# Own tile for sums of weights, later splits of new operands and next weights split a step ahead, in a one-core decoder layer

## The chip, the cores and the metric

The kernel runs on one core of a Trainium2 chip. The metric is the device time of one execution in microseconds, and the time of a kernel is the median of several executions. The engines named below are PE (matrix products), DVE (elementwise on tensors), ACT (activations, copies and casts), POOL, and SP, whose queue starts most of the DMA transfers. Each engine works through its own instructions strictly in order, and a semaphore holds it where it needs what another engine or a transfer has not yet delivered.

## The reference

One layer of a hybrid decoder for a prompt of 1024 tokens and eight sample tokens that share the weights (together 1032 columns), width 1024, in fp32:

```python
xn = rmsnorm(x, norm_mix_w)
sc_b, sc_c, sc_x, z, xbc, dt, q, gates = split(xn @ w_in)
y_a = (sc_b * conv3(sc_c * sc_x)) @ w_sc_out
y_b = group_rmsnorm((ssd(silu(conv4(xbc)), dt, ...) + D * xs) * silu(z)) @ w_ssm_out
y_c = cross_attention(q, mem_k, mem_v) @ w_attn_o
x = x + (sigmoid(g_a) * y_a + sigmoid(g_b) * y_b + sigmoid(g_c) * y_c) @ w_merge_o
xn = rmsnorm(x, norm_ffn_w)
x = x + (silu(xn @ w_gate) * (xn @ w_up)) @ w_down      # hidden width 2816
y = rmsnorm(x, norm_final_w)
```

For the sample tokens the state-space part (`ssd`) is one step of a recurrence over a state of 32 x 64 x 128 for each of the eight samples, which is read, updated and written back. The memory keys and values, the convolution histories and the states are outputs too.

## The kernel before

Every fp32 operand is split into a high part, which the matrix engine takes without loss, and a low part, the rest. ACT casts the high part (`S.copy`) and DVE subtracts it from the source (`V.tensor_sub`). A product is the sum of three matmuls: high with high, high with low, low with high.

The large matrix products go through `strassen()`, which makes two blocks of 128 output rows in one **step**: instead of eight half products it takes seven, named after the form of the moving operand that each uses: B11, T1, nT2, B21, T3, B22 and T4. Each product is 24 matmuls. The forms are sums of halves of the activations, made and split once and kept in SBUF for many steps. The weights are loaded per step as two raw tiles (`raw1`, `raw2`, by `st_raw`) and split (`st_split`) in four ways: A (raw1 itself, for B11 and B21), S (a first sum, in the tile `sa`, for T1 and nT2), T (a second sum, for T3 and B22) and D (half of raw2, for T4). The second sum is made by `st_adds2`, which writes it over raw1. Three PSUM tiles (m0 to m2) take turns: the copies to SBUF (`first`, L311) and the additions (L359, L371, L374, L381) empty them for the products that follow. In the steps of the first stage and of the hidden layer, a step's outputs are copied by ACT (L311) first.

Steps are named after what they make. In the first stage, C, B, X, G and Z stand for parts of `w_in`'s columns; X steps feed a convolution on DVE, which with its slots runs beside the next G step. The sample states run in the same stage: L859 loads a state tile `st`, L867 scales it on ACT (eight instructions a tile), L869 and L873 update and reduce it on DVE, L881 stores it. In the feed-forward stage, steps g0 to g20 and u0 to u20 make the gate and up halves of the 22 blocks of hidden rows. d00 to d06 and d10 to d16 are the down projection, with the first 1024 hidden rows and then with the second 1024; the last six blocks go another way (h_d).

The forms of the first 2048 hidden rows lie in DRAM (`hf_d`). `h_form` loads one form's two tiles of 128x1032 into event tiles and splits them into the tiles of activations: in u20 for d00 and again in d06 for d10. It is called by `used(f)`, as soon as the product with form f has been written down, since the new form takes the tiles of the old one. Pools: three raw, three high and three low weight tiles, twelve tiles a kind for the activations, five event tiles (`ev`), eight big tiles (which hold the outputs of steps and the residual x3).

The order of instructions on an engine comes from a scheduler that estimates when things are ready, not from the order of the source; `tick()` and `in_turn` only add constraints. Transfers of SP's queue start in order too: one that waits for a buffer holds up those behind it.

## Time and profile before

| | us |
|---|---|
| median of 3 runs | 2505.39 (2504.51 to 2506.88) |
| profiled execution, its own time | 2509.08 |
| its span | 2505.8 |
| PE busy in the span | 2434.5 (97%) |
| DVE busy | 1596.0 (64%) |
| ACT busy | 1070.7 (43%) |

The profiled execution lies 3.28 us above its span and 3.69 us above the median of the three runs. PE's busy time is the sum of its matmuls as the trace models them; the time of a step is read from the start of its first matmul to that of the next step's first one. A row of a timeline has the start in us, the length, the engine, the line, the operation with the tiles it writes and reads, and in brackets how long the engine had been idle and what released it.

### The profile page before, as it was taken

Reading aid. Unit: us, or ns where it says so; the run is one execution under the profiler, and the core shown is the slowest. Engines: PE = TensorE matmul, PEld = TensorE weight load, DVE = VectorE, ACT = ScalarE, POOL = GpSimd, SP = SyncE. Lnnn points to the kernel's source line nnn. Section 1 sums busy time; section 2 is a strip of 40 time slices with the busy share of each in tenths; the row PEclk is TensorE's granted clock in tenths of the full one; section 3 lists DMA queues with packets and bytes.
Section 4 is the critical chain, followed back from the end, with each engine's and each line's share of the span. In section 5 each row is a group of like instructions: output and inputs, shape, how many; then the busy total and the mean of one; then the engine's idle time right before and its main releaser. Section 6 shows DMA issues by size and latency. Waiting matters only on the chain.

```text
span 2505.8 us, 45588 instructions
## 1 busy us (share of the span) xinstructions
PE 2434.5 (97%) x18906; PEld 2315.8 (92%) x18906; DVE 1596.0 (64%) x2598; ACT 1070.7 (43%) x1716; POOL 116.3 (5%) x163
## 2 busy tenths in 40 slices
PE   7999999999999999999999989999999999999998
PEld 5899999999999999888888877899999999989998
DVE  5754586777677674656767562454777556566655
ACT  6554455354545435556544441223443333343222
POOL 0200010000000000221120000000000000000000
PEclk9999999999999999999999999999999999999999
DMA  6345434334344446567878677765444323274321
GB/s 197 106 128 167 131 107 145 114 117 127 124 127 128 134 150 209 171 214 253 265 230 283 202 262 237 263 235 158 149 158 127 110 89 111 68 268 141 100 85 68
DMA packets 356077, 404.80 MB, mean 162 GB/s; under 512 B 16422, under 2 KB 286870, under 8 KB 355863
## 3 DMA queue, kind: packets, MB, share of 16 engines
q1 hardware_dynamic: 335422, 344.18, 44.0%
q10 hardware_dynamic: 20449, 57.71, 5.9%
q8 instruction: 148, 2.42, 0.4%
q14 instruction: 58, 0.48, 0.1%
HBM read 286.74 MB, written 115.32 MB: 160 GB/s over the span
## 4 chain that ended last, share of the span: by engine, by line
PE 56%; DMA 4%; DVE 3%; ACT 1%; issue 1%; SPq 0%; ACTq 0%; DVEq 0%
PE po L214 12%; PE pm L1738 4%; PE ps_q L214 3%; PE pd L214 1%; PE py L981 1%; PE pss L994 1%; PE po L973 1%; PE d00m L260 1%; PE d10m L260 1%; PE Z14m L260 1%; PE G16m L260 1%; PE B6m L260 1%; PE C7m L260 1%; PE d16m L260 1%; PE d14m L260 1%; PE d02m L260 1%
## 5 line engine op out<-in xcount | busy, mean ns | idle before, releaser
L926 ACT ACTIVATE r<-r,acum 128x128 f32<-128x128 f32 x256 | 79.1, 391 | 3.8 <-DMA r<-ac_d 3.3
L867 ACT ACTIVATE st<-st,es 128x128 f32<-128x128 f32 x128 | 41.6, 394 | 61.4 <-DMA st<-in_state_ssm_dram 51.5
L697 DVE SCALAR_TENSOR_TENSOR ax<-u,prm,ax 128x1024 f32<-128x1024 f32 x44 | 56.3, 1280 | 0.0
L958 POOL TENSOR_TENSOR xdd<-xdt,decst 128x512 f32<-128x512 f32 x32 | 38.9, 1216 | 288.3 <-DVE xdt L954 288.3
L1385 DVE TENSOR_TENSOR yr<-po,yr 128x1032 f32<-128x1032 f32 x8 | 9.8, 1231 | 55.9 <-PE po L214 45.9
L977 DVE TENSOR_TENSOR y<-po,ea 128x512 f32<-128x512 f32 x28 | 19.3, 689 | 37.8 <-PE po L973 37.8
L952 DVE TENSOR_TENSOR r<-r,cbm 128x1024 f32<-128x1024 f32 x32 | 39.2, 1224 | 2.4
L869 DVE SCALAR_TENSOR_TENSOR st<-sr,dts,st 128x128 f32<-128x128 f32 x128 | 39.4, 345 | 0.4
L951 ACT COPY bT<-bp 128x128 f32<-128x128 f32 x32 | 8.5, 266 | 69.7 <-DVE cbm L949 69.5
L1950 ACT ACTIVATE fj<-psy 128x512 f32<-128x512 f32 (+1 forms) x18 | 10.7, 596 | 59.0 <-PE psy L1948 58.9
L981 PE MATMUL py<-r,xdt 128*64 128x128 f32 x512 | 35.0, 279 | 0.0
L873 DVE SCALAR_TENSOR_TENSOR sr<-st,sr 128x128 f32<-128x128 f32 x128 | 34.4, 285 | 0.8
L927 ACT ACTIVATE r<-r 128x1024 f32<-128x1024 f32 x32 | 33.8, 1057 | 0.6
L954 DVE TENSOR_TENSOR xdt<-xp,dtT 128x512 f32<-128x512 f32 x32 | 21.9, 684 | 19.0 <-PE xp L947 18.8
L1745 DVE TENSOR_TENSOR x<-pm,xT 128x516 f32<-128x516 f32 x16 | 11.1, 695 | 35.1 <-PE pm L1738 35.1
L994 PE MATMUL pss<-xdd,bT 128*128 128x512 f32 x64 | 33.3, 602 | 0.0
L766 ACT ACTIVATE ax<-ax 128x1032 f32<-128x1032 f32 x22 | 23.5, 1068 | 19.5 <-DVE ax L700 19.4
L981 PEld LDWEIGHTS py<-r,xdt 128*64 128x64 f32 x512 | 27.3, 136 | 4.2 <-issue 0.5
L973 PE MATMUL po<-bc,s 128*128 128x128 f32 x224 | 29.7, 275 | 1.0 <-DVE s L1000 1.0
L1007 POOL TENSOR_TENSOR s<-s,cdec 128x512 f32<-128x512 f32 x28 | 30.2, 1080 | 7.3 <-DVE s L1000 6.6
L973 PEld LDWEIGHTS po<-bc,s 128*128 128x128 f32 x224 | 27.6, 191 | 2.7 <-issue 1.6
L1667 DVE TENSOR_TENSOR gt<-po,gt 128x1032 f32<-128x1032 f32 x8 | 9.8, 1230 | 30.0 <-PE po L214 27.8
(9065 smaller groups left out, 9013.2 us busy)
## 6 DMA issues: line engine op xcount, KB each, us to landing
r<-ac_d SPq DMA_DIRECT2D x32, 512.0 KB
gt<-gt_d SPq DMA_DIRECT2D x24, 516.0 KB
xs_d<-ax ACTq DMA_DIRECT2D x22, 516.0 KB
gt_d<-G ACTq DMA_DIRECT2D x20, 516.0 KB
x<-xs_d SPq DMA_DIRECT2D x16, 516.0 KB
zs<-zs_d SPq DMA_DIRECT2D x16, 516.0 KB
yb_d<-x SPq DMA_DIRECT2D x16, 516.0 KB
in<-yb_d SPq DMA_DIRECT2D x16, 516.0 KB
```

What stands on the lines that cost most here:

```text
L214: PE.matmul(out[:, c : c + n], wt[:, ks], x[:, c : c + n], start=(k == 0 and i == 0), stop=(k == nk - 1 and i == 2),)
L260: PE.matmul(hv(ps)[:, c : c + n], wt[:, ks], x[:, c : c + n], start=(start and kt == 0 and i == 0), stop=(kt == 3 and i == 2), skip_group_ ...
L697: V.scalar_tensor_tensor(acc[:, :T], u[:, j : j + T], w[j], acc[:, :T], op0=ALU.mult, op1=ALU.add)
L867: S.activation(st[:, i], st[:, i], AF.Copy, scale=es[:, g * 4 + i, b : b + 1])
L869: V.scalar_tensor_tensor(st[:, i], rb, dts[:, g * 4 + i, b : b + 1], st[:, i], op0=ALU.mult, op1=ALU.add)
L926: S.activation(r[:, j, :], r[:, j, :], AF.Relu, scale=-1.0, bias=acum[:, c, h : h + 1])
L952: V.tensor_tensor(r, r, bc(cbm.unsqueeze(1), [P, HPG, P]), op=ALU.mult)
L958: G.tensor_tensor(b3(xdd, HPG), b3(xdt, HPG), bc(decst[:, c, hs].unsqueeze(2), [P, HPG, 64]), op=ALU.mult)
L973: PE.matmul(po[:, t * P : (t + 1) * P], state["s"][:, t * P : (t + 1) * P], bcg[1][:, cs], start=True, stop=True,)
L981: PE.matmul(py[hp : hp + 64, (h // 2) * P : (h // 2 + 1) * P], xdt[:, h * 64 : (h + 1) * 64], r[:, (h % 2) * 4 + h // 2, :], start=True, s ...
L994: PE.matmul(pss, bT, xdd, start=True, stop=True)
L1738: PE.matmul(hv(ps)[:, c : c + n], wt[:, ks], x[:, half * HT + c : half * HT + c + n], start=(k == 0 and i == 0), stop=(k == KD - 1 and i = ...
```

## The change

Five parts. (1) `st_adds2` writes the second sum into a tile of its own, `sb`, from the event tiles, and leaves raw1 as it is; the T split reads `sb`. (2) `used(f)` no longer splits at once: `h_form` starts the loads and returns a function that splits, and `turning` keeps these until three more products are done (`LATE`). Those left over at the end of a step are called in the next one. (3) `h_form` loads straight into the tile of the low part, casts the high part from there and subtracts in place; no event tile is taken, and the load waits until PE has read the tile's old content. (4) `following`: u20 and d06 load the first raw tile of the next step (named u20f and d06f) and make its A split (u20F, d06F), and `ahead` hands both to that step. Their D split stands ahead of T3. (5) The product of g20 and u20 with its two stores moves into d00 (`opening`, called as its `hook`), with the instruction that reads PSUM first, and so do four of the eight loads of the residual; the other four are ahead of d00.

```diff
...
 LAG = 3
+LATE = 3
...
         V.tensor_add(sa[:, 512:], sa[:, :512], raw1[:, :512])
         return raw1, raw2, sa, st_split(sa, f"{nm}S")
-    def st_adds2(raw1, raw2, sa):
-
-        V.tensor_add(raw1[:, :512], raw1[:, :512], raw2[:, :512])
+    def st_adds2(raw1, raw2, sa, nm, sums):
+        sb = sums(f"{nm}sb")
+        V.tensor_add(sb[:, :512], raw1[:, :512], raw2[:, :512])
         V.scalar_tensor_tensor(
-            raw1[:, 512:], sa[:, 512:], -1.0, raw1[:, 512:], op0=ALU.mult, op1=ALU.subtract
+            sb[:, 512:], sa[:, 512:], -1.0, raw1[:, 512:], op0=ALU.mult, op1=ALU.subtract
         )
-        return raw1
-
-    def st_sums2(raw1, raw2, sa, nm):
-        return st_split(st_adds2(raw1, raw2, sa), f"{nm}T")
+        return sb
+
+    def st_sums2(*args):
+        return st_split(st_adds2(*args), f"{args[3]}T")
+
+    ahead = []
+    turning = deque()
     def strassen(
-        src1, src2, forms, nm, sums, outs, early=None, after_t3=None, ready=None, hook=None, into=False, refill=None
+        src1, src2, forms, nm, sums, outs, early=None, after_t3=None, ready=None, hook=None, into=False,
+        refill=None, following=None,
     ):
...
                 S.copy(dst, ps)
         def used(f):
-            if refill is not None:
-                refill(f)
-
-
-        if ready is None and early is None:
+            turning.append(refill(f) if refill is not None else None)
+            if len(turning) > LATE:
+                g = turning.popleft()
+                if g is not None:
+                    g()
+
+
+        lead = ahead.pop() if ahead else None
+        if lead is not None:
+            raw1, raw2 = lead[0], st_raw(src2, f"{nm}r2")
+        elif ready is None and early is None:
             raw1, raw2 = st_raw(src1, f"{nm}r1"), st_raw(src2, f"{nm}r2")
...
         o11, o12, o21, o22 = outs()
         if early is None:
             pc = st_ps(tags[2], f"{nm}{tags[2]}")
-            wA = st_split(raw1, f"{nm}A")
+            wA = st_split(raw1, f"{nm}A") if lead is None else lead[1]
             prod(pa, wA, 0, "B11", True)
         else:
             tick()
...
             first(o11, hv(pa))
             used("B11")
         if ready is None:
-            sb = st_adds2(raw1, raw2, sa)
+            sb = st_adds2(raw1, raw2, sa, nm, sums)
...
             freed[0] = V.tensor_tensor(o12, hv(pa), o12, op=ALU.add).ins
         if ready is None:
             wT = st_split(sb, f"{nm}T")
+        if following is not None:
+            raw = st_raw(following, f"{nm}f")
+            wD = st_split(raw2[:, 512:], f"{nm}D", 512)
         tick()
         prod(pa, wT, 0, "T3", False)
         if after_t3 is not None:
...
         V.tensor_tensor(o12, o12, hv(pb), op=ALU.subtract)
         used("B22")
         tick()
-        wD = st_split(raw2[:, 512:], f"{nm}D", 512)
+        if following is None:
+            wD = st_split(raw2[:, 512:], f"{nm}D", 512)
+        else:
+            ahead.append((raw, st_split(raw, f"{nm}F")))
         prod(pa, wD, 0, "T4", False)
         used("T4")
         if into:
...
-    g0 = (*g0, st_sums2(*g0[:3], "g0"))
+    g0 = (*g0, st_sums2(*g0[:3], "g0", ev_sums))
...
         V.scalar_tensor_tensor(t2, t2, -1.0, b21, op0=ALU.mult, op1=ALU.subtract)
         form("T4", kt, t2)
-    def hidden_pair(nm, j, refill=None):
+    def hidden_pair(nm, j, **turn):
         o = []
         e = early.get((nm, j))
...
         src = ffn[nm]
         pa = strassen(
-            ev_sums, outs, e, ready=g0 if (nm, j) == ("g", 0) else None, refill=refill,
+            ev_sums, outs, e, ready=g0 if (nm, j) == ("g", 0) else None, **turn,
         )
         return o[0], o[1], pa if e is None else pa
...
     def h_form(ch, f):
-        for i in range(2):
-            t = ev_tile(f"hf{ch}{f}{i}", (P, 2 * HT))
-            SY.dma_start(t, hf_d[ch, FORMS.index(f), i])
-            mk = fx.get(f) or act_pair
-            hi, lo = mk("ah", f"h{ch}{f}{i}h"), mk("al", f"h{ch}{f}{i}l")
-            split_to(hi, lo, t.rearrange("p (a c) -> p a c", a=2))
+        mk = fx.get(f) or act_pair
+        pairs = [(mk("ah", f"h{ch}{f}{i}h"), mk("al", f"h{ch}{f}{i}l")) for i in range(2)]
+        for i, (hi, lo) in enumerate(pairs):
+            SY.dma_start(f32(lo), hf_d[ch, FORMS.index(f), i].rearrange("p (a c) -> p a c", a=2))
             hforms[ch][f] += [(hi[:, a], lo[:, a]) for a in range(2)]
+
+        def split():
+            for hi, lo in pairs:
+                S.copy(hi, f32(lo))
+                V.tensor_sub(lo, f32(lo), f32(hi))
+
+        return split
+
+    def w_rows(ch, m):
+
+        src = a["w_ffn_down"][0, ch * 1024 : (ch + 1) * 1024, m * P : (m + 1) * P]
+        return src.rearrange("(k t p) c -> p t k c", t=2, p=P)
     hs = {}
     for j in range(0, NF, 2):
...
         S.activation(s1, s1, AF.Silu)
         S.activation(s2[:, HS[1]], s2[:, HS[1]], AF.Silu)
         S.activation(s2[:, HS[0]], pa, AF.Silu, scale=-1.0)
-        u1, u2, pa = hidden_pair("u", j, (lambda f: h_form(0, f)) if j == NF - 2 else None)
-        V.tensor_mul(s1, s1, u1)
-        V.tensor_mul(s2[:, HS[1]], s2[:, HS[1]], u2[:, HS[1]])
-        V.scalar_tensor_tensor(s2[:, HS[0]], pa, -1.0, s2[:, HS[0]], op0=ALU.mult, op1=ALU.mult)
+        turn = dict(refill=lambda f: h_form(0, f), following=w_rows(0, 0)) if j == NF - 2 else {}
+        u1, u2, pa = hidden_pair("u", j, **turn)
+
+        def product(j=j, s1=s1, s2=s2, u1=u1, u2=u2, pa=pa):
+            V.scalar_tensor_tensor(s2[:, HS[0]], pa, -1.0, s2[:, HS[0]], op0=ALU.mult, op1=ALU.mult)
+            V.tensor_mul(s1, s1, u1)
+            V.tensor_mul(s2[:, HS[1]], s2[:, HS[1]], u2[:, HS[1]])
+            if j >= 16:
+                SY.dma_start(h_d[j - 16], s1)
+                SY.dma_start(h_d[j - 15], s2)
+
+        if j == NF - 2:
+            continue
+        product()
         if j >= 16:
-            SY.dma_start(h_d[j - 16], s1)
-            SY.dma_start(h_d[j - 15], s2)
             continue
         b11, b12, b21, b22 = (t[:, c] for t in (s1, s2) for c in HS)
         t1, t3, nt2, t4 = (t[:, c] for t in (u1, u2) for c in HS)
...
         kt = (j % 8) // 2
         for f, t in enumerate((b11, t1, nt2, b21, t3, b22, t4)):
             SY.dma_start(hf_d[j // 8, f, kt // 2][:, (kt % 2) * HT : (kt % 2 + 1) * HT], t)
-    def w_rows(ch, m):
-
-        src = a["w_ffn_down"][0, ch * 1024 : (ch + 1) * 1024, m * P : (m + 1) * P]
-        return src.rearrange("(k t p) c -> p t k c", t=2, p=P)
-
-    for m in range(KD):
-        x2[m] = big(f"x3_{m}")
-        SY.dma_start(x2[m], x2_d[m])
+    def residual(*ms):
+        for m in ms:
+            x2[m] = big(f"x3_{m}")
+            SY.dma_start(x2[m], x2_d[m])
+
+    residual(0, 1, 2, 3)
+
+    def opening():
+        product()
+        residual(4, 5, 6, 7)
+
     for ch in range(2):
         for m in range(0, KD, 2):
+            turn = dict(refill=lambda f: h_form(1, f), following=w_rows(1, 0)) if ch == 0 and m == KD - 2 else {}
             strassen(
                 w_rows(ch, m), w_rows(ch, m + 1), hforms[ch], f"d{ch}{m}", ev_sums,
                 lambda m=m: (x2[m][:, HS[0]], x2[m][:, HS[1]], x2[m + 1][:, HS[0]], x2[m + 1][:, HS[1]]),
-                into=True, refill=(lambda f: h_form(1, f)) if ch == 0 and m == KD - 2 else None,
+                into=True, hook=opening if ch == 0 and m == 0 else None, **turn,
             )
     st_stack.close()
     pmm[0] = ctx.enter_context(tc.tile_pool(name="pmm2", bufs=2, space=PSUM))
```

Three places in the order of instructions follow, rows as they stand before and after. A name with a number is one buffer; x4 means four alike in a row.

The first place is step C0 of the first stage, on ACT. `c` and `su` are its outputs, `st` the state tiles, C0Th and C0Dh the high parts of its T and D splits. Before:

```order
L247 CAST C0Th<-C0r_4649 128x1024
L817 DMA gt_d<-G_4415 128x1032
L311 COPY c_4655<-C0m_4653 128x516
L867 ACTIVATE st_5231<-st_5231,es 128x128 x4
L311 COPY su_4656<-C0m_4654 128x516
L867 ACTIVATE st_5231<-st_5231,es 128x128 x2
L867 ACTIVATE st_5700<-st_5700,es 128x128
L247 CAST C0Dh<-C0r_4651 128x512
L311 COPY c_4655<-C0m_4653 128x516
L867 ACTIVATE st_5700<-st_5700,es 128x128 x7
```

After:

```order
L248 CAST C0Th<-C0sb 128x1024
L834 DMA gt_d<-G_4427 128x1032
L316 COPY c_4668<-C0m_4666 128x516
L884 ACTIVATE st_5247<-st_5247,es 128x128 x4
L316 COPY su_4669<-C0m_4667 128x516
L884 ACTIVATE st_5247<-st_5247,es 128x128 x3
L248 CAST C0Dh<-C0r_4664 128x512
L316 COPY c_4668<-C0m_4666 128x516
L884 ACTIVATE st_5718<-st_5718,es 128x128 x4
```

The D cast and the second copy of c now stand ahead of the first activation on the second state tile; all eight activations of the first state tile are ahead of them.

The same place on SP: the loads of weights C0r, C1r and of the states, and the stores of older ones. Before:

```order
L241 DMA C0r_4651<-in_w_in_dram 128x8x128
L881 DMA out_s_ssm_dram<-st_4457 128x4x128 x2
L859 DMA st_5231<-in_state_ssm_dram 128x4x128
L241 DMA C1r_4863<-in_w_in_dram 128x8x128
L859 DMA st_5231<-in_state_ssm_dram 128x4x128
L881 DMA out_s_ssm_dram<-st_4613 128x4x128 x2
L241 DMA C1r_4865<-in_w_in_dram 128x8x128
L859 DMA st_5700<-in_state_ssm_dram 128x4x128 x2
```

After:

```order
L242 DMA C0r_4664<-in_w_in_dram 128x8x128
L898 DMA out_s_ssm_dram<-st_4470 128x4x128 x2
L242 DMA C1r_4877<-in_w_in_dram 128x8x128
L876 DMA st_5247<-in_state_ssm_dram 128x4x128 x2
L242 DMA C1r_4879<-in_w_in_dram 128x8x128
L898 DMA out_s_ssm_dram<-st_4626 128x4x128 x2
L876 DMA st_5718<-in_state_ssm_dram 128x4x128 x2
```

Both loads of the first state tile now stand behind C1's first weights, and C1's second weights ahead of the stores.

The second place is DVE at the change from u20 to d00. h0... are the splits of the new forms, d00A/u20F the A split, x_0 and x_1 the residual. The piece before starts with the last splits of forms:

```order
L390 TENSOR_TENSOR h0T40l<-hf0T_23851,h0T40h 128x2x516
L390 TENSOR_TENSOR h0T41l<-hf0T_23857,h0T41h 128x2x516
L1850 TENSOR_TENSOR g20o_23374<-g20o_23374,u20o_23581 128x1032
L1851 TENSOR_TENSOR g20o_23375<-g20o_23375,u20o_23582 128x516
L1852 SCALAR_TENSOR_TENSOR g20o_23375<-u20m_23579,g20o_23375 128x516
L248 TENSOR_TENSOR d00Al<-d00r_23884,d00Ah 128x1024
L340 TENSOR_TENSOR d00sa<-d00r_23887 128x512
L341 TENSOR_TENSOR d00sa<-d00sa,d00r_23884 128x512
L293 TENSOR_TENSOR d00r_23884<-d00r_23884,d00r_23887 128x512
L294 SCALAR_TENSOR_TENSOR d00r_23884<-d00sa,d00r_23884 128x512
L248 TENSOR_TENSOR d00Sl<-d00sa,d00Sh 128x1024
```

After, from u20's subtraction of B22 to the next splits:

```order
L388 TENSOR_TENSOR u20o_23642<-u20o_23642,u20m_23641 128x516
L1861 TENSOR_TENSOR h0B211l<-h0B211l,h0B211h 128x2x516
L249 TENSOR_TENSOR d00Sl<-d00sa,d00Sh 128x1024
L1861 TENSOR_TENSOR h0T30l<-h0T30l,h0T30h 128x2x516
L1861 TENSOR_TENSOR h0T31l<-h0T31l,h0T31h 128x2x516
L1880 SCALAR_TENSOR_TENSOR g20o_23435<-u20m_23640,g20o_23435 128x516
L1881 TENSOR_TENSOR g20o_23434<-g20o_23434,u20o_23642 128x1032
L1882 TENSOR_TENSOR g20o_23435<-g20o_23435,u20o_23643 128x516
L1861 TENSOR_TENSOR h0B220l<-h0B220l,h0B220h 128x2x516
L1861 TENSOR_TENSOR h0B221l<-h0B221l,h0B221h 128x2x516
```

and from there, without a gap, to d02's A split:

```order
L314 TENSOR_TENSOR x_0_23906<-d00m_23917,x_0_23906 128x516
L1861 TENSOR_TENSOR h0T40l<-h0T40l,h0T40h 128x2x516
L314 TENSOR_TENSOR x_1_23908<-d00m_23918,x_1_23908 128x516
L1861 TENSOR_TENSOR h0T41l<-h0T41l,h0T41h 128x2x516
L249 TENSOR_TENSOR d00Tl<-d00sb,d00Th 128x1024
L314 TENSOR_TENSOR x_0_23906<-d00m_23917,x_0_23906 128x516
L370 TENSOR_TENSOR x_0_23906<-d00m_23919,x_0_23906 128x516
L249 TENSOR_TENSOR d00Dl<-d00r_23914,d00Dh 128x512
L385 TENSOR_TENSOR x_1_23908<-x_1_23908,d00m_23917 128x516
L388 TENSOR_TENSOR x_0_23906<-x_0_23906,d00m_23918 128x516
L398 TENSOR_TENSOR x_1_23908<-x_1_23908,d00m_23917 128x516
L249 TENSOR_TENSOR d02Al<-d02r_24138,d02Ah 128x1024
```

The A split, d00's sums and its S split have gone ahead of the forms T3 to T4, the product stands in the middle of these splits, and the T split stands at their end. d02's A split stands behind the last subtraction of d00 (L398).

The third place is DVE in step G6, beside the convolution of X6 (ax, L697 to L700 before). Before:

```order
L697 SCALAR_TENSOR_TENSOR ax_6006<-u_5806,prm,ax_6006 128x1024
L698 SCALAR_TENSOR_TENSOR ax_6020<-h_xc,prm,ax_6020 128x8
L700 SCALAR_TENSOR_TENSOR ax_6006<-u_5806,prm,ax_6006 128x1032
L697 SCALAR_TENSOR_TENSOR ax_6020<-u_5807,prm,ax_6020 128x1024
L248 TENSOR_TENSOR G6Tl<-G6r_6031,G6Th 128x1024
L697 SCALAR_TENSOR_TENSOR ax_6020<-u_5807,prm,ax_6020 128x1024
L869 SCALAR_TENSOR_TENSOR st_6092<-sr_6090,dts,st_6092 128x128
L700 SCALAR_TENSOR_TENSOR ax_6020<-u_5807,prm,ax_6020 128x1032
L869 SCALAR_TENSOR_TENSOR st_6092<-sr_6090,dts,st_6092 128x128 x7
```

After:

```order
L714 SCALAR_TENSOR_TENSOR ax_6025<-u_5824,prm,ax_6025 128x1024
L715 SCALAR_TENSOR_TENSOR ax_6039<-h_xc,prm,ax_6039 128x8
L717 SCALAR_TENSOR_TENSOR ax_6025<-u_5824,prm,ax_6025 128x1032
L714 SCALAR_TENSOR_TENSOR ax_6039<-u_5825,prm,ax_6039 128x1024
L294 TENSOR_TENSOR G6sb<-G6r_6050,G6r_6052 128x512
L714 SCALAR_TENSOR_TENSOR ax_6039<-u_5825,prm,ax_6039 128x1024
L295 SCALAR_TENSOR_TENSOR G6sb<-G6sa,G6r_6050 128x512
L717 SCALAR_TENSOR_TENSOR ax_6039<-u_5825,prm,ax_6039 128x1032
L886 SCALAR_TENSOR_TENSOR st_6112<-sr_6110,dts,st_6112 128x128 x5
L249 TENSOR_TENSOR G6Tl<-G6sb,G6Th 128x1024
```

The two sums (sb) come later than the S split, and the T split stands behind the last instructions of the convolution and five updates of a state.

## The prediction

> **What bounds the kernel now.** I read the page's busy times first, then the waits of PE, then windows cut at the starts of single steps, and last the timelines of the engines that PE waits for.
>
> ```profile
> span 2505.8 us, 45588 instructions
> PE 2434.5 (97%) x18906; PEld 2315.8 (92%) x18906; DVE 1596.0 (64%) x2598; ACT 1070.7 (43%) x1716; POOL 116.3 (5%) x163
> ```
>
> PE is busy for 97% of the span, and the change does not alter its number of matmuls. What can be won are PE's stops, 2505.8 − 2434.5 = 71 us in all, and the slow matmuls that follow a long stop. The stops that the change can touch are these (engine, tile and line that waits, what it waits for, us in total, times, longest):
>
> ```profile
> PE d00m L260 <- DVE g20o L1852: 5.9, 1, 5.9
> ...
> PE d10m L260 <- DVE x L381: 3.5, 1, 3.5
> ...
> PE C6m L260 <- ACT c L311: 2.7, 1, 2.7
> ...
> PE C2m L260 <- ACT c L311: 2.0, 1, 2.0
> PE C0m L260 <- ACT c L311: 2.0, 1, 2.0
> PE d10m L260 <- DVE d10Al L248: 2.0, 1, 2.0
> ...
> PE C4m L260 <- ACT c L311: 1.5, 1, 1.5
> ...
> PE X8m L260 <- ACT u L311: 0.4, 1, 0.4
> ...
> PE X12m L260 <- ACT u L311: 0.3, 1, 0.3
> ```
>
> The waits are less than what the stops cost. Windows that run from one step's first matmul to the next one's (columns: window, its length, busy time of PE, weight loads, DVE, ACT and POOL, then granted clock, DMA share, GB/s) are, for u20, d00, d02, d06 and d10:
>
> ```profile
> 2213.04:2232.96 19.92, 19.92 (x170) 19.92 (x169) 17.10 (x17) 17.03 (x20) 0.00 (x0) 1.00 0.87 293
> 2232.96:2262.12 29.16, 23.22 (x171) 22.81 (x169) 21.14 (x26) 6.56 (x8) 0.00 (x0) 0.82 0.69 236
> 2262.12:2282.04 19.92, 19.92 (x170) 19.92 (x169) 11.54 (x15) 3.78 (x4) 0.00 (x0) 1.00 0.18 53
> 2301.97:2321.90 19.93, 19.93 (x171) 19.93 (x169) 18.50 (x20) 15.03 (x15) 0.00 (x0) 1.00 0.85 273
> 2321.90:2350.50 28.60, 23.11 (x170) 22.70 (x169) 20.22 (x25) 6.92 (x7) 0.00 (x0) 0.88 0.22 69
> ```
>
> A step without a stop takes 19.92 us, 2.85 for each of its seven products. d00 takes 29.16, a loss of 9.24 on 5.94 of waiting; d10 takes 28.60, a loss of 8.68 on 5.5. The rest is the clock, 0.82 and 0.88 in these windows. PE's timeline (start, length, then the instruction) shows it at d00:
>
> ```profile
> 2233.20 0.40 PE L260 MATMUL d00m<-h0B110l,d00Ah 128*128 128x256 f32 x2
> 2239.54 0.80 PE L260 MATMUL d00m<-h0B210h,d00Ah 128*128 128x256 f32 x2 [5.94 <-DVE g20o L1852]
> 2240.14 0.63 PE L260 MATMUL d00m<-h0B210l,d00Ah 128*128 128x256 f32 x2
> ```
>
> In the same way for one undisturbed step of the first stage, and C0, C2, C4 and C6:
>
> ```profile
> 402.88:422.87 19.99, 19.99 (x170) 19.99 (x169) 19.26 (x48) 11.45 (x14) 1.07 (x2) 1.00 0.52 159
> 422.87:446.65 23.78, 21.78 (x170) 21.58 (x169) 13.79 (x33) 12.31 (x26) 1.24 (x2) 0.93 0.45 135
> 566.96:589.22 22.26, 20.25 (x171) 20.04 (x169) 13.70 (x33) 12.11 (x27) 1.23 (x2) 1.00 0.49 142
> 710.26:732.00 21.74, 20.24 (x170) 20.04 (x169) 13.70 (x33) 11.85 (x25) 1.23 (x2) 1.00 0.49 146
> 852.50:877.16 24.66, 21.91 (x170) 21.50 (x169) 13.78 (x33) 13.20 (x27) 1.23 (x2) 0.93 0.45 138
> ```
>
> Over 19.99 these lose 3.79, 2.27, 1.75 and 4.67, together **12.48**. C0 and C6, with stops of 2.0 and 2.7, also lose clock (0.93); C4 with 1.5 does not.
>
> **Why C0 waits.** Timelines of ACT, SP and DVE:
>
> ```profile
> 435.00 0.40 ACT L867 ACTIVATE st<-st,es 128x128 f32<-128x128 f32 x1 [5.05 <-DMA st<-in_state_ssm_dram]
> 435.81 0.58 ACT L311 COPY c<-C0m 128x516 f32<-128x516 f32 x1
> 429.76 0.38 SPq L241 DMA_DIRECT2D C1r<-in_w_in_dram  x1
> 430.39 0.93 SPq L859 DMA_DIRECT2D st<-in_state_ssm_dram  x2
> 428.51 1.22 DVE L248 TENSOR_TENSOR C0Tl<-C0r,C0Th 128x1024 fp32r<-128x1024 f32 x1
> ```
>
> The copy of c that lets PE write T3 stands on ACT behind a state activation, which sat 5.05 us for its load. That load stood on SP behind the second load of C1's weights, which waited for a raw tile; and the tile was held until DVE's T split at 428.51 to 429.73 had read it, because the sums of weights lay in it.
>
> **The change: own tile for sums.** The T split now reads the sum tile, so a raw tile comes free two or more us earlier. More surely, ACT's order is turned: in C0 the copy of c and the D cast stand ahead of the first st_5718 activation (before: st_5700 ahead of both). The wait for that load now falls behind the copy, with nothing of this step queued behind it but C1's A cast, needed only at the next step. The other state tile (st_5247) has both its halves loaded behind C1's first weights; it is used ahead of the su copy, and by SP's order its load should land before ACT comes to it. The four places have one pattern, and I take the whole **−12.5** there. Bounds: nothing gained (the other activation inherits the wait), and 12.5. X8 and X12 have the same turn: their waits of 0.4 and 0.3 go, **−0.7**.
>
> What it costs: the sums are two instructions as before, but their tile must come from five event tiles, and DVE's order puts the T split later in X and G steps, the first-stage ones with convolution work. For G2:
>
> ```profile
> 407.36 1.22 DVE L248 TENSOR_TENSOR G2Tl<-G2r,G2Th 128x1024 fp32r<-128x1024 f32 x1
> 409.96 1.28 DVE L700 SCALAR_TENSOR_TENSOR ax<-u,prm,ax 128x1032 f32<-128x1032 f32 x1
> 411.16 2.11 DVE L869 SCALAR_TENSOR_TENSOR st<-sr,dts,st 128x128 f32<-128x128 f32 x7
> 414.77 0.40 PE L260 MATMUL G2m<-xnh,G2Tl 128*128 128x256 f32 x2
> ```
>
> The split ends at 408.58, and PE reads it at 414.77, 6.2 us later. In the new order (the G6 rows of the section on the change) one more convolution instruction, the last one of the convolution, and five state updates stand ahead of it: 1.2 + 1.2 + 5 × 0.3 = 3.9 us. That leaves 2.3 us, so I charge nothing as forecast; what hides it is the products T1 to B21. For small new waits, where such margins are thinner (X0, g0, u0), I set **+0.7** (bounds 0 and 3).
>
> **The change: h splits and d weights.** Before, DVE came to d00 with the splits of h, the product with u20 and only then d00's A split:
>
> ```profile
> 2237.05 1.23 DVE L1850 TENSOR_TENSOR g20o<-g20o,u20o 128x1032 f32<-128x1032 f32 x1
> 2238.19 0.69 DVE L1851 TENSOR_TENSOR g20o<-g20o,u20o 128x516 f32<-128x516 f32 x1
> 2238.80 0.69 DVE L1852 SCALAR_TENSOR_TENSOR g20o<-u20m,g20o 128x516 f32<-128x516 f32 x1
> ```
>
> The starts give DVE's prices: 1.14 for a split or a wide product, 0.6 for half of one. Now u20Fl (the A split) stands far ahead, the STT that frees PSUM comes first of the three product instructions, and the T3, B22 and T4 splits of h fall in d00, whose DVE ends on the T split and the add of x_0 that reads nT2's PSUM (row 1992 of the order). Counted from u20's start: B22 ends at 6 × 2.85 = 17.1. From there to row 1992 stand ten instructions of 1.14 and six of 0.6, 15.0 us, so DVE is done at 32.1, or 32.7 if the first starts 0.6 late. PE comes to T3 after 106 of d00's 168 matmuls, at 19.92 × (1 + 106/168) = 32.5. The STT is done at 17.1 + 5.8 = 22.9 and B21, which needs its PSUM, comes at 19.92 + 5.7 = 25.6. So d00's stop goes from 9.24 lost to about 0.6 (bounds 0 and 2): **−8.6**. It keeps a margin near zero, and what is late next is this DVE chain.
>
> The loads are under it. Each h load now waits until PE has left its tile, two per product. A load alone took:
>
> ```profile
> 2212.54 0.34 SPq L1837 DMA_DIRECT2D hf0nT<-hf_d  x1
> ...
> GB/s 0 0 0 0 0 0 264 116 231 380 380 413 297 33 0 0 66 8 82 195 260 313 326 330 334 154 181 153 252 351 415 297 330 182 248 83 215 248 281 363
> GB/s 0 0 303 427 344 385 385 413 344 372 413 413 330 372 427 413 372 358 372 399 179 14 14 61 38 99 79 82 167 130 154 160 123 160 215 307 341 341 348 376
> ```
>
> (the strips have 40 slices; the first, from 2212, of 0.25 us; the second, from 2115, of 0.15 us and with stores in the same 2064-byte pieces that the new loads use). The load was issued at 2212.54 and had landed by 2215.3, 2.75 us. Two of 528 KB per 2.85 us ask for 371 GB/s, and the second strip shows 330 to 427. Then the last one, T41, issued at about 20.0, lands near 22.9, while DVE, after ten more instructions behind B22, comes to it at 29.2. At 300 GB/s it would land at 27 and x_0 behind it at 28.8, where DVE wants x_0 at 26.9: a stop of some 2 us, the upper bound above.
>
> d10 goes the same way: its A split (d06Fl), sums and S split stand ahead of d10; x_7's last subtraction, for which it waited 3.5, no longer has a split of T4 ahead of it. By the same count d10Tl is done at 30.3 and wanted at 31.8. I leave 0.2 of 8.68: **−8.5** (bounds 0 and 2 of stop).
>
> One wait is new: d02Al now stands behind x_1's last subtraction of d00, which reads T4. T4 ends with d00, 0.6 + 1.2 us later the split is ready, and PE has 8 matmuls, 0.95 us, to do without it. With a semaphore's delay: **+1.3** (bounds 0 and 2). The copies of product and stores moved into d00 are in the count; the loads of x_4 to x_7 queue on SP behind the two stores, and d04 wants them a step later, so they cost nothing.
>
> Sum: −8.6 − 8.5 + 1.3 − 12.5 − 0.7 + 0.7 = **−28.3**. The profiled run took 2509.1, 3.3 around its span, and 3.7 above the median of 2505.4. It gives 2480.8, and by the median **2477**.
>
> **The rule weighed here.** The rows say that a stop of 2.0 us (C0) already cost 3.79, with the clock at 0.93, and 1.5 (C4) only 1.75. The Trainium skill, "TensorE: Matmul & The Clock Gate", Part 1, has the clock fall to half after an idle window of about 3.4 us, free-running. By it the stops of 0.6 and 1.3 that I leave cost themselves alone, as by C4's row, and a stop of 2 us would too, where C0's row makes it 3.8; the row decides.
>
> **Rivals.** *The state wait only moves (0.2).* st_5247's activation, which stands ahead of the su copy, inherits C0's wait, and its like in the other three. For it: the load is issued from the same in-order queue. Against: the raw tile is free earlier. Then 12.5 is not won: 2489.5.
>
> *The chase of loads fails (0.15).* The h loads start only when PE leaves their tiles, and DVE has no margin at d00. If d00 and d10 each stop for 2 us, C0's price is 3.8 each, in place of 0.8 together: +6.8, 2484. By the Trainium skill's rule above ("TensorE: Matmul & The Clock Gate", Part 1) it would be 4.0 together, some 2480.
>
> *Nothing is won in all (0.04).* Both of these happen with longer stops, 5 us in each of the two steps: the change doesn't do what it says, about 2505.
>
> *Slower (0.05).* The T split in the 16 X and G steps waits for an event tile. The margin is 2.3; from 4.4 us of delay on, each stops for 2.1 or more, 16 × 2.1 = 34, more than all gains. With 2.4 each it is 38: 2515. Against it: five tiles, and a sum is read within a few us.
>
> **How the numbers follow.** The forecast has 0.56. From the bounds, its own range is 2474 (none of the new stops, 2.8 less) to 2484. The range goes down to 2472, since the three runs before lie 2.4 apart, and up to 2491, which takes in the moved state wait. A measurement tells 0.2%, 5 us, from no change. Faster by more: 0.56 + 0.2 + 0.15 = 0.91; within: 0.04; slower: 0.05.
>
> **What would show it.** PE's waits: no c copy in C0 to C6, no g20o at d00, no x at d10; d00 and d10 at 20 to 21 us with the clock at 1.00; d02 at 21.2, waiting for d02Al. The forecast is wrong if C steps still take over 22, if X and G steps show T-split waits, or if d00's stop names an h load.

## The result and the profile after

The changed kernel takes **2482.63 us** (median of 4 runs, 2481.25 to 2484.12), the kernel before in the same comparison 2506.14 (2504.51 to 2509.74): a ratio of 0.9904, 95% interval 0.9887 to 0.9922, or 23.5 us. The profiled run took 2481.99, its span 2480.1; against the span before that is 25.7 less.

The page of the changed kernel:

```profile
span 2480.1 us, 45608 instructions
PE 2426.3 (98%) x18906; PEld 2308.0 (93%) x18906; DVE 1587.2 (64%) x2598; ACT 1072.3 (43%) x1716; POOL 118.3 (5%) x163
```

PE's waits in it that answer to those shown of before (engine, tile and line that waits, what for, us in total, times, longest):

```profile
PE d00m L261 <- DVE x L314: 1.2, 1, 1.2
PE d06m L261 <- DVE x L385: 1.2, 1, 1.2
...
PE d02m L261 <- ACT d02Ah L248: 0.7, 1, 0.7
...
PE X0m L261 <- DVE X0Tl L249: 0.6, 1, 0.6
...
PE X8m L261 <- DVE u L385: 0.3, 1, 0.3
PE d10m L261 <- DVE d10Tl L249: 0.3, 1, 0.3
...
PE u20m L261 <- DVE u20o L385: 0.3, 1, 0.3
```

No C step waits any more, and the long stops of d00 and d10 are gone; short ones stand in u20, d00, d02, d06 and d10. Those in u20, d02 and d06 are new, and only d02's was forecast. Windows from one step's first matmul to the next one's, for C0, C6, u20, d00, d02, d06 and d10 (columns as in the prediction):

```profile
423.23:443.22 19.99, 19.99 (x170) 19.99 (x169) 12.97 (x36) 10.78 (x25) 1.23 (x2) 1.00 0.53 160
...
843.78:863.77 19.99, 19.99 (x170) 19.99 (x169) 12.99 (x36) 10.79 (x25) 1.23 (x2) 1.00 0.52 159
2199.07:2219.52 20.45, 20.16 (x170) 19.98 (x169) 15.12 (x18) 14.87 (x19) 0.00 (x0) 1.00 0.85 296
2219.52:2242.25 22.73, 20.66 (x171) 20.03 (x169) 17.48 (x21) 7.49 (x9) 0.00 (x0) 1.00 1.02 358
2242.25:2262.81 20.56, 20.51 (x169) 20.25 (x170) 15.65 (x22) 4.77 (x6) 0.00 (x0) 1.00 0.29 84
2282.73:2304.08 21.35, 20.18 (x171) 20.00 (x169) 17.46 (x22) 13.53 (x15) 0.00 (x0) 1.00 0.86 292
2304.08:2324.79 20.71, 20.38 (x170) 20.10 (x169) 19.74 (x23) 7.86 (x9) 0.00 (x0) 1.00 0.53 156
```

The granted clock is 1.00 in all of them. C0, C2, C4 and C6 together fall from 92.44 to 79.97 us, 12.47 less. Against before, u20 is 0.53 longer, d00 6.43 shorter, d02 0.64 and d06 1.42 longer, and d10 7.89 shorter: 11.73 less together. The two groups are 24.2 of the 25.7.

Why d00 takes 22.73 us, 2.8 more than a step without a stop, is seen on DVE. Its timeline in the changed kernel, at the points that the prediction counted from (u20 starts at 2199.07):

```profile
2205.37 1.23 DVE L1861 TENSOR_TENSOR h0B110l<-h0B110l,h0B110h 128x1032 fp32r<-128x1032 f32 x1 [3.26 <-ACT h0B110h L1860]
2208.05 1.24 DVE L1861 TENSOR_TENSOR h0B111l<-h0B111l,h0B111h 128x1032 fp32r<-128x1032 f32 x1 [1.44 <-ACT h0B111h L1860]
2209.78 1.23 DVE L1861 TENSOR_TENSOR h0T10l<-h0T10l,h0T10h 128x1032 fp32r<-128x1032 f32 x1 [0.49 <-ACT h0T10h L1860]
...
2218.66 0.68 DVE L388 TENSOR_TENSOR u20o<-u20o,u20m 128x516 f32<-128x516 f32 x1
...
2228.47 0.69 DVE L314 TENSOR_TENSOR x<-d00m,x 128x516 f32<-128x516 f32 x1
...
2233.10 0.68 DVE L314 TENSOR_TENSOR x<-d00m,x 128x516 f32<-128x516 f32 x1
```

and PE's, at the end of u20's B22:

```profile
2215.92 0.40 PE L261 MATMUL u20m<-B222h,u20Tl 128*128 128x256 f32 x2
2216.60 0.47 PE L261 MATMUL u20m<-T40h,u20Dh 128*128 128x256 f32 x2 [0.29 <-DVE u20o L385]
```

DVE waits, through ACT's casts, for the first three loads of h, and from 2209.78 to 2233.78 it has hardly a gap. PE ends B22 at 2216.3, 17.2 us after u20's start, as counted; B22's subtraction comes on DVE at 2218.66, 2.3 us later. From there to the end of the last row shown are 15.1 us, as counted; the whole chain begins late.

### The profile page after: what moved, and what is told of

Its sections match the earlier page's. It is cut to its first block, busy times and chain, and to the rows that moved or that the text cites. A ratio compares the mean times of both kernels' runs of the same rounds, so it can differ in the third digit from the quotient of the medians.

```text
span 2480.1 us, 45608 instructions
## 1 busy us (share of the span) xinstructions
PE 2426.3 (98%) x18906; PEld 2308.0 (93%) x18906; DVE 1587.2 (64%) x2598; ACT 1072.3 (43%) x1716; POOL 118.3 (5%) x163
## 4 chain that ended last, share of the span: by engine, by line
PE 86%; DMA 6%; DVE 4%; ACT 2%; issue 1%; SPq 0%; ACTq 0%; POOL 0%; DVEq 0%
PE po L215 12%; PE pm L1755 4%; PE ps_q L215 3%; PE pd L215 1%; PE py L998 1%; PE ps_g L215 1%; PE pss L1011 1%; PE po L990 1%; PE Z2m L261 1%; PE C3m L261 1%; PE G18m L261 1%; PE Z14m L261 1%; PE C6m L261 1%; PE G12m L261 1%; PE C4m L261 1%
## 5 line engine op out<-in xcount | busy, mean ns | idle before, releaser
L717 DVE SCALAR_TENSOR_TENSOR ax<-u,prm,ax 128x1032 f32<-128x1032 f32 x22 | 28.3, 1287 | 0.0
```

## The experiments

All are compared by steps as well as by time, since the medians of the kernel before differ by 4 us from one comparison to the next. The sums (us) are of the steps' lengths in the trace; without a stop they would be 79.97, 59.76 and 39.85. Each sum comes from one profiled execution. The four kernels that do not touch the d steps (before, own_tile_alone, order_alone, own_tile_order_back) differ among themselves by 1.6 and 0.8 us in the last two columns; with the short stops of the changed kernel the scatter looks smaller (d06 and d10 take 41.77 to 42.06 in the changed kernel, no_opening and weights_first).

| kernel | median | ratio to before, 95% interval | C0, C2, C4, C6 | u20, d00, d02 | d06, d10 |
|---|---|---|---|---|---|
| before | 2506.14 | | 92.44 | 69.00 | 48.53 |
| changed | 2482.63 | 0.9904 (0.9887 to 0.9922) | 79.97 | 63.74 | 42.06 |
| own_tile_alone | 2492.74 | 0.9950 (0.9934 to 0.9966) | 79.99 | 69.88 | 48.68 |
| order_alone | 2499.72 | 0.9979 (0.9966 to 0.9991) | 86.05 | 68.31 | 47.91 |
| own_tile_order_back | 2503.94 | 0.9992 (0.9983 to 1.0002) | 90.81 | 69.11 | 48.22 |
| no_opening | 2485.46 | 0.9921 (0.9904 to 0.9939) | 79.98 | 68.59 | 41.77 |
| splits_at_once | 2490.16 | 0.9923 (0.9902 to 0.9943) | 79.98 | 69.59 | 45.46 |
| no_opening_at_once | 2488.43 | 0.9916 (0.9895 to 0.9937) | 79.97 | 66.95 | 43.99 |
| event_tile_loads | 2479.98 | 0.9893 (0.9878 to 0.9908) | 79.99 | 62.93 | 40.50 |
| no_following | 2483.54 | 0.9909 (0.9893 to 0.9925) | 79.98 | 64.31 | 41.86 |
| own_late_opening | 2480.72 | 0.9888 (0.9864 to 0.9912) | 79.96 | 63.22 | 40.89 |
| splits_behind_add | 2480.89 | 0.9893 (0.9875 to 0.9911) | 79.97 | 63.82 | 40.84 |
| weights_first | 2479.99 | 0.9886 (0.9870 to 0.9903) | 79.99 | 62.39 | 41.79 |
| add_first_weights_first | 2477.88 | 0.9884 (0.9867 to 0.9901) | 79.98 | 60.98 | 40.63 |

**The first stage.** What ends the stops in the C steps: the order on ACT (theory O), or the raw tile that comes free earlier (theory R)?

```diff
 own_tile_alone: the kernel before with
+        sb = sums(f"{nm}sb")
+        V.tensor_add(sb[:, :512], raw1[:, :512], raw2[:, :512])
...
+        return sb
```

> The kernel before, with the own tile for the second sum and nothing else of the change. In ACT's order the second copy of c and the D cast of C0, C2, C4 and C6 stand ahead of the first activation on the second state tile, as in the changed kernel. Theory O (the order on ACT alone ends these stops): the four steps lose under 0.3 us each, so 12.5 us are gained there, d00 and d10 stay near 29 and 28.6 us, median 2493 (2491 to 2495). Theory R (the raw tile is free earlier, so SP issues the state load earlier): the same median, but the load of the second state tile is issued less than 7.5 us into C0; theory O has it no earlier than before. If the gain hangs on the rest of the change: 2506.

Measured: the whole 12.45, and d00 and d10 as before. So part 1 carries the first stage alone. But the second state tile's load is issued at 433.70, 9.4 us into C0, which is later than the 7.5 of before. Its cause is the row ahead of it on SP:

```profile
423.63 0.37 SPq L241 DMA_DIRECT2D C1r<-in_w_in_dram  x1
426.05 5.67 SPq L881 DMA_DIRECT2D out_s_ssm_dram<-st  x2
433.70 0.93 SPq L859 DMA_DIRECT2D st<-in_state_ssm_dram  x2
```

The stores of the older state wait for DVE and hold up the load; C1's second weights, which wait for the raw tile, have moved ahead to 423.63, 0.7 us before C0's start at 424.30. In the changed kernel it is the same pattern, and ACT still waits for the load of the second state tile, now behind the copy of c. The activations on the first one (x4) wait for nothing:

```profile
426.75 1.28 ACT L884 ACTIVATE st<-st,es 128x128 f32<-128x128 f32 x4
...
432.26 0.58 ACT L316 COPY c<-C0m 128x516 f32<-128x516 f32 x1
435.84 1.28 ACT L884 ACTIVATE st<-st,es 128x128 f32<-128x128 f32 x4 [3.00 <-DMA st<-in_state_ssm_dram]
```

```diff
 order_alone: the kernel before, with the sums in raw1, and
-                S.copy(dst, ps)
+                last[nm] = S.copy(dst, ps).ins      # for C0: in the end the second copy of c
...
-            S.activation(st[:, i], st[:, i], AF.Copy, ...)
+            ins = S.activation(st[:, i], st[:, i], AF.Copy, ...)
+            c = {6: "C0", 14: "C2", 22: "C4", 30: "C6"}.get(n)
+            if c is not None:
+                tc.add_manual_dep(ins.ins, last[c].name, ...)
 own_tile_order_back: own_tile_alone, and in the same places
...
+            if i == 0 and c is not None:
+                tc.add_manual_dep(last[c], ins.ins.name, ...)
```

> The kernel before with the sums still in raw1; the only edit is an order on ACT: the first activation on the second state tile stands behind the second copy of c in C0, C2, C4 and C6. SP's order is that of before. Theory O: the four steps lose under 0.5 us each, median 2493.6 (2492 to 2496). Theory R: nothing is gained, since the state load is as late as before and some other wait takes its place: 2506.

> The kernel before with the own tile, and the order on ACT turned back: the second copy of c stands behind the first activation on the second state tile in C0, C2, C4 and C6. Theory O: the four stops are back, 10 to 16 us together, median 2503 to 2509. Theory R: they stay away, 2493.

Order alone brings half: 6.4 of 12.5. Some 3.3 of it are shorter stops (8.2 us in the four steps of before, 4.9 here); the rest is the slow matmuls of C0 and C6 in before, since no step of the four loses clock here. No C step waits for the copy of c any more, and another wait comes to light later in the step, at T4. Four rows of C0, from SP, DVE and PE:

```profile
427.96 0.38 SPq L241 DMA_DIRECT2D C1r<-in_w_in_dram  x1
432.34 0.69 DVE L342 TENSOR_TENSOR C1sa<-C1r 128x512 f32<-128x512 f32 x1 [4.41 <-DMA C1r<-in_w_in_dram]
...
436.42 1.23 DVE L248 TENSOR_TENSOR C1Al<-C1r,C1Ah 128x1024 fp32r<-128x1024 f32 x1 [1.45 <-ACT C1Ah L247]
...
439.63 0.50 PE L260 MATMUL C0m<-T40ah,C0Dh 128*128 128x256 f32 x2 [1.68 <-DVE su L373]
```

C1's second weights still wait for the raw tile. DVE stands 4.41 us at the sum that needs them, with C0's D split and the subtractions that free PSUM behind it, and then 1.45 us more for ACT's cast of C1's A split; PE waits for these. The other way round, the own tile with the order turned back has most of the loss again, 10.84 over 79.97, so that it brings 1.6 by itself:

```profile
434.29 0.40 ACT L869 ACTIVATE st<-st,es 128x128 f32<-128x128 f32 x1 [3.44 <-DMA st<-in_state_ssm_dram]
434.59 0.57 ACT L313 COPY c<-C0m 128x516 f32<-128x516 f32 x1
...
435.21 0.53 PE L260 MATMUL C0m<-xnh,C0Th 128*128 128x256 f32 x2 [1.93 <-ACT c L313]
```

Neither theory alone holds: two waits stood one behind the other. The order on ACT takes away the first, and the own tile, which brings this order too, also takes away the second. That it does so through C1's weights, which get a raw tile 0.7 us before C0 starts, is how I read these rows; no run moves those weights alone.

**The change of operands.** Which parts carry d00 and d10?

```diff
 no_opening: the changed kernel with
-        if j == NF - 2:
-            continue
         product()
...
-    residual(0, 1, 2, 3)
+    residual(*range(KD))
...
-                into=True, hook=opening if ch == 0 and m == 0 else None, **turn,
+                into=True, **turn,
 splits_at_once: the changed kernel with
-LATE = 3
+LATE = 0
 no_opening_at_once: both edits
```

> The changed kernel without part 5: the product of g20 and u20, its two stores and all eight residual loads stand in the program ahead of d00. DVE's order then has d00Tl and all splits of h ahead of the first addition of x_0, which nT2 of d00 waits for. Theory D (the stop left in d00 is the length of DVE's chain, started late and then without a gap): counted by the changed kernel's starts (2218.66, ten of 1.14 and four of 0.6) the addition ends 4.5 us after PE wants it, in place of 1.4, with slow matmuls behind it: d00 takes 26 to 30 us instead of 22.7, median 2485.5 to 2490. Theory L (the stop is the loads of h, which come late): d00 stays at 22.7, median 2482.6.

> The changed kernel without part 2: the splits of h stand in the program where their loads do (LATE = 0). The scheduler orders by when things are ready, and its order on ACT stays the same but for one row; on DVE the S split of d00 comes behind three more splits, and the addition of x_0 earlier. Counted from the changed kernel's 2218.66: S split done at 2223.9 where T1 wants it at 2222.9 (stop 1.0), PSUM freed by the product's first instruction at 2226.2 where B21 wants it near 2226 (0 to 1). d00 22 to 23.5, median 2482.6 within 1.5: part 2 alone is worth nothing. If part 2 carries the gain: ACT and DVE wait for loads ahead of u20's copies and additions, u20 or d00 lose 3 us or more, 2486 or more.

> The changed kernel without parts 2 and 5 (own tile, direct loads and next weights ahead remain). In DVE's order d00's S split stands behind the product and all but one split of h. Counted from 2218.66: done at 2228.4, where T1 wants it at 2222.9; a stop of 5.5 us, with slow matmuls behind it as at d00 of the kernel before. Theory D (DVE's order in u20 and d00 is what the d steps gained): d00 27 to 30, and the gain there is nearly all given back, median 2487 to 2491. If the direct loads or the early weights carry the gain: d00 stays under 25, 2482 to 2485.

no_opening: u20, d00 and d02 lose 4.85, nearly all of what they had gained; d10 keeps its gain. PE waits 3.1 us for the addition of x_0 that was forecast to be 4.5 late. d00 itself takes 26.3, and the median, 2485.46, is at the low edge of what theory D gave.

splits_at_once: "worth nothing" was wrong, by far. Both groups lose, 5.85 and 3.40. PE's two stops in u20 to d02:

```profile
2218.86 0.51 PE L261 MATMUL u20m<-T40h,u20Dh 128*128 128x256 f32 x2 [1.80 <-DVE u20o L385]
2245.40 0.50 PE L261 MATMUL d02m<-h0B110h,d02Ah 128*128 128x256 f32 x2 [3.31 <-ACT d02Ah L248]
...
2197.89:2223.35 25.46, 23.66 (x187) 23.46 (x185) 20.02 (x22) 16.86 (x21) 0.00 (x0) 0.93 0.83 288
```

The first is DVE's subtraction of T3 in u20, which now stands behind three splits of h; I had counted only the rows from B22 on, and it lies ahead of them. This stop, of 1.80 us, also costs clock: 0.93 in the window shown last, from u20's start. The second is d02's weights, behind four residual loads, behind the product's stores, behind the product, whose instructions stand between splits.

no_opening_at_once: by the figures that were forecast, theory D holds: d00 takes 28.6 (27 to 30) and the median is 2488.43 (2487 to 2491), though PE waits 2.1 us ahead of T1 and not 5.5, since it had already lost time in u20. By the sums it does not hold. The window of d00 begins early here, with d00's first matmul 17.3 us into u20, ahead of u20's T4, so it can't be set beside the 29.16 of before. u20, d00 and d02 together keep 2.05 of the 5.26 us that the changed kernel gained there, d06 and d10 keep 4.54 of 6.47: more than half of the gain is left where "nearly all" was to be given back. The own tile alone gained nothing in these steps, so the direct loads, the early weights or both are worth something when the other two parts are missing; no run tells which.

```diff
 event_tile_loads: the changed kernel, h_form as before but for the late split
+            srcs.append(ev_tile(f"hf{ch}{f}{i}", (P, 2 * HT)))
+            SY.dma_start(srcs[-1], hf_d[ch, FORMS.index(f), i])
...
+                split_to(hi, lo, t.rearrange("p (a c) -> p a c", a=2))
 no_following: the changed kernel with
...                              # in u20 and d06, the loads and the A split of the next step:
-    , following=w_rows(0, 0)
-    , following=w_rows(1, 0)
 own_late_opening: both edits
```

> The changed kernel without part 3: h comes through the five event tiles again, in pieces of 4128 bytes, ahead of the splits. The sums of d00's weights need event tiles too, so in DVE's order they and the S split stand behind the product, in d00. Theory P (part 3 is worth what it frees: the event tiles, so that sums and S split run early): d00 stops ahead of T1 and takes 24 to 28, d10 22 to 26, median 2486 to 2492. Rival (the direct loads in small pieces, which wait for PE, cost more than they bring): d00 at 21.5 or less, 2481 or less.

> The changed kernel without part 4: the raw loads and A splits of d00 and d10 belong to their own steps again. In the scheduler's order they stand almost where u20f and d06f stood (loads ahead of the h loads, the A split of d00 in the same row of DVE), so by the order nothing is lost: d00 22 to 23.5, d10 20 to 21.5, median 2482.6 within 1.5. If part 4 carries the gain: d00 and d10 lose the A split and its cast behind the h splits again, 2 us or more each, 2486 or more.

> The changed kernel without parts 3 and 4: own tile, splits three products on, and the opening in d00; h comes through event tiles, and weights and A splits belong to their own steps. The order on DVE is that of event_tile_loads but for the A split. If these three parts are the whole gain: d00 22 to 24, d10 20 to 21.5, median 2480 (2478.5 to 2482). If part 3 or 4 is needed once the other is gone: d00 or d10 2 us or more above that, 2483 or more.

event_tile_loads: theory P fell. The rival's median came (2479.98, with 2481 or less forecast), its d00 did not: that takes 22.78, nearly as with the direct loads, but for other reasons:

```profile
PE d00m L261 <- ACT d00Sh L248: 1.3, 1, 1.3
...
PE d00m L261 <- DVE d00Tl L249: 1.0, 1, 1.0
```

The sums are late, as expected, but the stop ahead of T1 is only 1.3; on the other hand h is split earlier (its first split starts 2.7 us into u20, 6.3 in the changed kernel), so that u20 (19.93) and d06 (19.92) have no stop. By the steps it is 2.4 us better than the changed kernel; the intervals of the times overlap. no_following is the changed kernel within a microsecond: the scheduler puts the loads and the split in nearly the same places. own_late_opening has the whole gain with three parts of five. So parts 3 and 4 bring nothing that can be seen as long as parts 2 and 5 are there; parts 2 and 5 can carry the d steps with the own tile alone, and each without the other, beside parts 3 and 4, loses nearly all or all of the gain in u20 to d02.

**What is left.** Three orders on top of the changed kernel, with no work added:

```diff
 splits_behind_add (held[0]: the last addition to x that empties PSUM)
+                with nullcontext() if behind is None or f not in ("T3", "B22", "T4") else tc.issue_after(behind):
                     V.tensor_sub(lo, f32(lo), f32(hi))
 weights_first: in the changed kernel, opening() is cut in two
     def opening():
         product()
-        residual(4, 5, 6, 7)
+    def second():                # d02's hook
+        residual(4, 5, 6, 7)
 add_first_weights_first: both, and in d06 the nT2 splits behind x_7's subtraction of T3
```

> The changed kernel with one order more on DVE: in d00 and d10 the T3, B22 and T4 splits of h stand behind the addition to x that empties PSUM for the next product (B11's, T1's, nT2's); in the scheduler's order this brings the T split ahead of them too. No work is added or taken away. Theory D (what is left in d00 is DVE's chain, begun 2 us late, with the addition of x_0 behind seven splits and sums): from 2218.66 the addition now comes after 7.0 us instead of 10.4, at 26.0 us of u20's time where nT2 wants it at 28.2; the stops of 1.2 and 0.2 go, d00 falls from 22.7 to 20.0 to 21.0 (d02's late weights stay in it), d06 stays at 21.3, about 2 us in all: 2480.6 (2479 to 2482). Theory L (late loads of h are the stop): the loads are the same, d00 stays at 22.5 or more, 2482.6.

> The changed kernel with one edit: the loads of x_4 to x_7 stand in d02's hook instead of d00's, so that on SP d02's weights stand ahead of them. Theory W (d02 waits for weights that queue behind four residual loads, which wait for the stores of the product): d02's cast no longer waits 12.5 us for its load, the stop of 0.7 ahead of d02 goes, and u20, d00 and d02 together take 62.4 to 62.9 us instead of 63.74; d00's own stops (1.2 and 0.2) stay; median 2481.5 (2480.5 to 2482.5). If d02's split, behind d00's last subtraction on DVE, is late anyway: 63.4 or more.

> As splits_behind_add, and two more orders: the residual loads x_4 to x_7 stand in d02's hook, so that d02's weights come ahead of them on SP, and in d06 the nT2 splits of h stand behind x_7's subtraction of T3. By theory D with its two companions (d02 waits for weights behind the residual's loads, d06 for a subtraction behind two splits): d00 at 20.0 to 20.4, d02 at 20.0 to 20.3, d06 at 20.0 to 20.5, d10 at 20.7 or less; 4 us less than the changed kernel, 2478.5 (2477 to 2480.5). If d06's stop comes from T4's loads of weights or from PE, d06 stays at 21.3. If DVE's whole load is the limit, what d06 gains d10 loses.

splits_behind_add: the chain was shortened as counted, T split and all, but the steps u20 to d02 stayed at 63.82; d00 at 22.47 is a miss for theory D alone. The median, 2480.89, fell into the forecast range all the same, by luck: the 1.2 us that this kernel's steps are shorter lie in d06 and d10. DVE, ACT and PE of this kernel show what took its place:

```profile
2224.67 1.22 DVE L249 TENSOR_TENSOR d00Tl<-d00sb,d00Th 128x1024 fp32r<-128x1024 f32 x1
2227.84 0.70 DVE L315 TENSOR_TENSOR x<-d00m,x 128x516 f32<-128x516 f32 x1 [1.96 <-DMA x<-x_d]
...
2241.66 1.04 ACT L248 CAST d02Ah<-d02r 128x1024 fp32r<-128x1024 f32 x1 [9.53 <-DMA d02r<-in_w_ffn_down_dram]
...
2228.59 0.51 PE L261 MATMUL d00m<-h0nT20h,d00Sh 128*128 128x256 f32 x2 [0.55 <-DVE x L315]
2242.76 0.51 PE L261 MATMUL d02m<-h0B110h,d02Ah 128*128 128x256 f32 x2 [1.07 <-ACT d02Ah L248]
```

DVE had reached the addition by 2225.9 and then waited for the load of x_0, which queues behind 14 loads of h; and d02's cast ended no earlier than before, since its weights landed no earlier, so PE only waited there longer. weights_first takes this second wait away by itself: u20 to d02 at 62.39, as expected, with d00's own stops of 1.2 and 0.2 unchanged; its median, 2479.99, lies 0.5 below the forecast range, with runs from 2475.58 to 2484.30. But DVE's order changed with it. The A split of d02, which in the changed kernel stood behind x_1's last subtraction (L398), now stands ahead of it:

```profile
2241.66 1.22 DVE L249 TENSOR_TENSOR d02Al<-d02r,d02Ah 128x1024 fp32r<-128x1024 f32 x1
...
2245.55 0.69 DVE L398 TENSOR_TENSOR x<-x,d00m 128x516 f32<-128x516 f32 x1 [0.27 <-PE d00m L261]
```

So this run takes both causes of d02's wait away at once, the late weights and the late subtraction. no_opening has the second alone: its residual loads wait for no product, its weights land in time, the cast is done at 2241.1, long before d02's first matmul at 2245.59, and the split stands behind the subtraction. There d02 takes 21.39, 1.5 more than a step without a stop:

```profile
2245.79 0.69 DVE L398 TENSOR_TENSOR x<-x,d00m 128x516 f32<-128x516 f32 x1 [2.15 <-PE d00m L261]
2246.40 1.22 DVE L249 TENSOR_TENSOR d02Al<-d02r,d02Ah 128x1024 fp32r<-128x1024 f32 x1
```

With all three orders d00 and d02 have no wait of PE above 0.2 us, d06 takes 19.98, and the kernel, add_first_weights_first, has the lowest median of all: the steps are 4.2 us shorter than the changed kernel's (forecast 4), the median 4.75. (Its d00 and d02 windows, 17.49 and 23.05, count only together, 40.54: one pair of d02's matmuls stands ahead of d00's T4.) PE's longest waits left in these steps:

```profile
PE d10m L261 <- DVE d10Sl L249: 0.4, 1, 0.4
...
PE u20m L261 <- DVE u20o L385: 0.3, 1, 0.3
```

Its interval still overlaps the changed kernel's, so that the steps, not the times, tell the two apart.

## Why the prediction was right, and where it was not

- **First stage, −12.5:** measured −12.47. The size was right and the reason half right. "The T split now reads the sum tile, so a raw tile comes free" is true, and matters for C1's second weights and DVE; it does not bring the state load forward, which comes 2 us later than before. ACT's order, on which the step leaned "more surely", does the other half. The rival in which the wait only moves named the first state tile's activation, ahead of the su copy; that one waits for nothing. The second tile's activation keeps its wait, 3.00 us, behind the copy of c, where PE does not feel it.
- **X8 and X12, −0.7:** X12 gains 0.54, X8 nothing (20.69 after 20.65), X4 0.35 that was not counted.
- **d00, −8.6:** measured −6.43. The step that failed is "B22 ends at 6 × 2.85 = 17.1. From there to row 1992": the 15.0 us are right, the start is not, because DVE was behind with the splits of h, which had begun late. The first load, issued at 2200.45, let ACT begin its cast at 2204.28, 3.8 us later and not 2.75. That much of the rival in which the chase of loads fails did happen. I also asked for the wrong end: T3 has the last instruction of the chain, but nT2 needs the addition of x_0 (row 1987), and stopped 1.2 us for it.
- **d02, +1.3:** 0.64 in its own window and some 0.8 at the end of d00's. The size is about right, the cause was not only x_1's subtraction: "the loads of x_4 to x_7 ... cost nothing" overlooked that d02's weights queue behind them and keep ACT's cast waiting. The split behind the subtraction was late too, so that either would have stopped PE. no_opening shows the forecast mechanism by itself, at 1.5 us. The delay of a semaphore that the term allowed for isn't seen: in the changed kernel d02's A split ends at 2243.45 and PE reads it at 2243.51.
- **d06:** no term. Its stop of 1.2 (1.42 in the step), and 0.3 in u20, are the splits for the next operands ahead of a subtraction that frees PSUM; I had looked only at the step that uses the new operands, not at the one in which they are split.
- **d10, −8.5:** measured −7.89. What is left is 0.8 over a step without a stop, with one wait of 0.3 for the T split in it.
- **Small new waits, +0.7**, and the slower rival: X0, Z4 and others have waits of 0.6 or less, the span outside the two groups and X4 to X12 is 0.7 us shorter all the same, and no G step waits for its T split.
- **The median.** In the span the sum was −28.3 against −25.7 measured; for the profiled run the forecast was 2480.8, and it took 2481.99. That this looks closer is luck: the time of the profiled run lay 3.3 over its span before and 1.9 after. The median of 2482.63 lies 5.6 over the forecast of 2477, because I carried over the 3.7 us by which the profiled run of before lay above its median. The profiled run of after lies 0.6 below its own: that offset was scatter between runs.

Of the signs that it named, d00 at 20 to 21 us did not come (22.73), and d02 took 20.56 and not 21.2, with its longest wait for the cast and not for the A split; the others came. Of the signs that would have made it wrong there is one trace, X0's wait of 0.6 for its T split.

The margins that the prediction set between 0 and 2 for d00 and d02 were where the time went; the rival with 2 us of stop in d00 and d10, 2484, lies nearer to the median than the forecast does, though its stops (1.4 and 0.3 us) and its slow clock did not come like that.

On the rule of the clock: stops of 1.2 in d00 and d06 left the clock at 1.00. The Trainium skill, "TensorE: Matmul & The Clock Gate", Part 1, says the same of stops under its window of about 3.4 us.

## What to carry to other kernels

A long stop often has a second wait behind it: before counting a stop as won, follow what is queued on every engine and DMA queue behind the instruction that ended it, and where work is moved past a queue, what stands behind it there. On an engine that works in order, count a chain from where the engine really is, not from where its input is ready, and look at each instruction that frees PSUM for the one product that wants it. When a scheduler sets the order, a part of a change may do nothing by itself; undoing one part at a time tells which, and undoing two at once can show that a third stands in for them.
